# Elementwise work of a two-layer diffusion trunk moved from GpSimd to VectorE and ScalarE

## The chip, the cores and the metric
The kernel runs on one core of a Trainium2 chip. The core has TensorE (PE; its weight loads are PEld), VectorE (DVE), ScalarE (ACT), GpSimd (POOL) and SyncE (SP), which issues most DMAs; each works through its own queue in order. The metric is the device time of one execution in microseconds, and the time shown is the median of three runs.

## The reference
Two layers over 256 context and 256 latent tokens of width 1024. Each layer has four token mixers side by side (gated DeltaNet, S5, HGRN2, retention), each in two directions, then an output projection, a gate, a residual and a layer norm; then a channel mixer, dense SwiGLU in layer 0 and eight experts, two per token, in layer 1. Only latent tokens leave. What the change touches, cut to its core:

```
x  <- LN(alpha*x + gate*sublayer(mod(x)))                # norm, affine g and b
q, k, v = split(silu(short_conv(qkv)));  q = l2norm(q)*64**-.5;  k = l2norm(k)
S5:   lam_bar = exp(lam*step);  h_t = lam_bar*h_(t-1) + b_bar u_t;  y = Re(C h)   # complex
HGRN: att[i,j] = sum_k q[i,k] k[j,k] exp(g[i,k]-g[j,k]),  j <= i
MoE:  out = alpha*x + gate*sum_e w_e * (silu(h w1_e)*(h w3_e)) w2_e
```

## The kernel before
All matrices are fp32 and are multiplied in three passes: a weight arrives by DMA as `wraw`, ScalarE rounds it to `whi` (L390), VectorE or GpSimd subtracts to get `wlo` (L305), and TensorE adds xh*whi, xl*whi and xh*wlo. Tokens lie along the free dimension (512 in layer 0, 256 latent ones in layer 1), features over partitions in tiles of 128.

The stages follow one another: adaLN vectors and the modulated input (`xl`, `xh`); S5 tables, made on the chip from the parameters (`s5_tables`: powers of the step, input weights `s5W`, phases `s5res`, output tables C times a power, stored to DRAM and loaded back); projections and DeltaNet features; S5 states; retention; DeltaNet blocks and chain; HGRN attention by levels; output projection; norm; dense mixer; norm; the same mixers for layer 1; norm; experts. The tables of layer 1 are made beside the first norm.

The order of every engine's queue is set when the program is built: a scheduler walks the instructions by priority, and `tc.high_priority(n)` shifts that of a block. Tiles live in pools, entered and left, and rings of buffers (`bufs`). Names and lines in the rows: L305 is any two-operand product, sum or difference, L317 one with a scalar between, L321 and L323 one with scalars, L329 to L331 ScalarE's functions, L373 a matmul, L386 a weight's DMA. `s5a`, `s5b`, `s5Z`, `s5H` are the S5 states' products, sums and results (L1420 on), two directions one after the other; `hea` the exponents of an HGRN level (L1020 on); `lr`, `lnq`, `lnx` the norm's rows, its Newton step on the inverse root and its affine result; `mlo` the low part of an expert's unit of 1 MB (128x2048); `m_acc` the accumulator of the experts, filled with alpha times the normed rows (`moe_begin`), and `e_sel` the 0/1 matrix that gathers an expert's tokens. A silu is three functions on ScalarE and a last product, which here GpSimd does (L362).

Of the kernel before, what the change touches and what calls it, by code (L numbers as in the profile page):

```python
# [24 lines left out]
P = 128  # L25
# [205 lines left out]
class Trunk:  # L231
# [314 lines left out]
    def gdn_feat(self, l, grp, i, ps, s0, ns):  # L546
# [14 lines left out]
        self.mul(sq, y, y, eng=self.G)  # L561
# [443 lines left out]
    def hgrn_att(self, s, rings):  # L1005
# [8 lines left out]
        for n, sz in enumerate((128, 0) + HLEVELS):  # L1014
            if sz == 0:
                kl = self.t("hkl", [2, 256], bufs=2)
                self.add(kl, kf, kb, eng=self.G)
                ql = q
            else:
# [6 lines left out]
                self.sub(eq[:, :, :, 1], inc[:, :, :, 1], m(0), eng=self.G)  # L1026
                self.sub(eq[:, :, :, 0], m(1), exc[:, :, :, 0], eng=self.G)
# [162 lines left out]
    def s5_tables(self, l):  # L1190
        nc, G = self.nc, self.G
        e = G
# [3 lines left out]
        Ball, Call = n("B", 2, 16, 16), n("C", 3, 16, 16)  # L1196
# [66 lines left out]
        LW, LC = n("LW", 2, 16, 8), n("LC", 2, 16, 8)  # L1263
# [37 lines left out]
        for g0 in range(0, 16, 4):  # L1301
# [4 lines left out]
            sh = [P, 4, 8, 16]  # L1306
            lw = tuple(LW[:, c, gs, :, None].to_broadcast(sh) for c in range(2))
            wb = tuple(bb[:, c, :, None, :].to_broadcast(sh) for c in range(2))
            W = self.t("s5W", [2, 4, 16, 8], bufs=2)
            Wv = W.rearrange("p c g h j -> p c g j h")  # L1310
            tmp, tmq = (self.t(x, [4, 8, 16]) for x in ("s5tmp", "s5tmq"))
            self.cmul((Wv[:, 0], Wv[:, 1]), lw, wb, tmp)
# [16 lines left out]
            lc = tuple(LC[:, c, gs, :, None].to_broadcast(sh) for c in range(2))  # L1329
            cb = tuple(Cm[:, c, :, None, :].to_broadcast(sh) for c in range(3))  # L1330
            Y = self.t("s5W", [2, 4, 16, 8], bufs=2)
            Yv = Y.rearrange("p c g h i -> p c g i h")
            self.mul(Yv[:, 0], lc[0], cb[0], e)
            self.mul(tmq, lc[1], cb[1], e)
            self.sub(Yv[:, 0], Yv[:, 0], tmq, e)
            self.mul(Yv[:, 1], lc[0], cb[2], e)
            self.mul(tmq, lc[1], cb[0], e)
            self.sub(Yv[:, 1], Yv[:, 1], tmq, e)
            nc.sync.dma_start(scm[g0 // 4], Y.rearrange("p c g h i -> p (c g h i)"))
# [731 lines left out]
    def run(self):  # L2071
# [14 lines left out]
        with self.context("B"):  # L2086
            tables = self.s5_tables(1)
# [51 lines left out]
```

## Time and profile before

| | before |
|---|---|
| median of three runs (lowest, highest) | 2537.23 us (2534.49, 2539.19) |
| profiled execution | 2538.93 us, span 2537.1 us |
| busy TensorE | 2273.1 us, 90% |
| busy VectorE | 1735.0 us, 68% |
| busy ScalarE | 1265.9 us, 50% |
| busy GpSimd | 526.0 us, 21%, 494 instructions |
| mean granted TensorE clock | 0.926 |

Stages by time: tables, input and first projections to about 180 us; mixers of layer 0 to 585; norm and layer 1's tables to 642; dense mixer to 1020; norm to 1072; mixers of layer 1 to 1452; norm, router and gather to 1500; experts to 2520; last norm. A share of busy time over the whole span mixes these; what a part is worth is read from its own stretch.

### The profile page before, as it was taken

The page shows a single profiled execution, that of the slowest core. Times are in us where ns is not written, and L with a number is a line of the kernel's source. Part 1 is how long each engine was busy: PE and PEld are TensorE (multiplying, and loading weights), DVE is VectorE, ACT ScalarE, POOL GpSimd, SP SyncE. Part 2 cuts the span into 40 slices and gives each one's busy share as a digit, 9 for nine tenths or more (in the row PEclk, how much of TensorE's full clock was granted, in tenths as well). Part 3 has the DMA queues.
Part 4 walks back from the last instruction along what each step waited for, and adds up shares of the span by engine and source line. Part 5 has one row for each costly group of instructions (what it writes and reads, how often), then busy time and mean ns, then how long its engine had stood idle before and what let it go on. Part 6 is the DMA issues. An engine that isn't in the chain of part 4 may idle for free. (4 is left out here: it accounts for less than half of the span.)

```text
span 2537.1 us, 33303 instructions
## 1 busy us (share of the span) xinstructions
PE 2273.1 (90%) x12928; PEld 1781.8 (70%) x12928; DVE 1735.0 (68%) x2326; ACT 1265.9 (50%) x1459; POOL 526.0 (21%) x494
## 2 busy tenths in 40 slices
PE   3789998878999999789877769999999999999997
PEld 2567666554788887468656558778787878788885
DVE  7646556787533322454566588988888888889887
ACT  1443433322544422533533337767676767677774
POOL 5523433326422200332332230000000000001000
PEclk7889998888999999889987779999999999999998
DMA  7243142415422233652130439989898989899994
GB/s 287 95 154 104 59 172 85 154 57 185 169 99 100 90 126 108 230 168 91 63 122 14 183 142 353 360 311 362 321 366 313 364 322 365 309 358 339 367 361 169
DMA packets 122515, 532.75 MB, mean 210 GB/s; under 512 B 25968, under 2 KB 37232, under 8 KB 78960
## 3 DMA queue, kind: packets, MB, share of 16 engines
q1 hardware_dynamic: 95472, 511.74, 54.8%
q10 hardware_dynamic: 26880, 18.82, 2.5%
q8 instruction: 104, 1.70, 0.3%
q14 instruction: 59, 0.48, 0.1%
HBM read 509.23 MB, written 21.28 MB: 209 GB/s over the span
## 5 line engine op out<-in xcount | busy, mean ns | idle before, releaser
L305 DVE TENSOR_TENSOR mlo<-mraw,mhi 128x2048 fp32r<-128x2048 f32 x333 | 769.8, 2324 | 110.8 <-ACT mhi L390 108.8
L390 ACT CAST mhi<-mraw 128x2048 fp32r<-128x2048 f32 x336 | 639.2, 1906 | 216.0 <-PE psh L373 136.0
L373 PE MATMUL psh<-mlo,e_xh 128*128 128x512 f32 x896 | 358.4, 400 | 6.3 <-DVE mlo L305 6.3
L373 PE MATMUL psh<-mhi,e_xh 128*128 128x512 f32 x896 | 351.7, 395 | 7.8 <-ACT mhi L390 7.8
L373 PE MATMUL psh<-mhi,e_xl 128*128 128x512 f32 x896 | 352.3, 393 | 0.0
L373 PE MATMUL psacc<-xh,whi 128*128 128x512 f32 (+2 forms) x784 | 315.5, 403 | 35.5 <-ACT k2P L329 13.3
L390 ACT CAST whi<-wraw 128x1024 fp32r<-128x1024 f32 x142 | 145.5, 1026 | 352.9 <-PE psacc L373 335.3
L373 PE MATMUL psacc<-xh,wlo 128*128 128x512 f32 (+2 forms) x784 | 309.0, 394 | 9.2 <-DVE wlo L305 9.2
L373 PE MATMUL psacc<-xl,whi 128*128 128x512 f32 (+2 forms) x784 | 308.2, 393 | 6.5 <-DVE xl L305 6.4
L305 DVE TENSOR_TENSOR wlo<-wraw,whi 128x1024 fp32r<-128x1024 f32 x142 | 179.6, 1266 | 194.8 <-ACT whi L390 185.3
L305 POOL TENSOR_TENSOR e_xl<-k2B,e_xh 128x512 fp32r<-128x512 f32 x16 | 31.0, 1946 | 997.5 <-ACT e_xh L1867 997.5
L373 PEld LDWEIGHTS psacc<-xh,whi 128*128 128x128 f32 (+1 forms) x784 | 152.4, 195 | 73.6 <-ACT k2P L329 25.8
L373 PEld LDWEIGHTS psh<-mhi,e_xh 128*128 128x128 f32 x896 | 170.1, 190 | 46.3 <-ACT mhi L390 8.9
L373 PEld LDWEIGHTS psh<-mlo,e_xh 128*128 128x128 f32 x896 | 170.3, 190 | 43.6 <-DVE mlo L305 8.6
L373 PEld LDWEIGHTS psh<-mhi,e_xl 128*128 128x128 f32 x896 | 170.1, 190 | 34.3
L373 PEld LDWEIGHTS psacc<-xh,wlo 128*128 128x128 f32 (+1 forms) x784 | 151.5, 193 | 45.4 <-DVE wlo L305 11.3
L373 PEld LDWEIGHTS psacc<-xl,whi 128*128 128x128 f32 (+1 forms) x784 | 152.0, 194 | 42.4 <-DVE xl L305 8.7
L373 PE MATMUL psy<-mlo,e_gh 128*128 128x512 f32 x448 | 177.0, 397 | 0.0
L373 PE MATMUL psy<-mhi,e_gl 128*128 128x512 f32 x448 | 173.9, 391 | 0.0
L373 PE MATMUL psy<-mhi,e_gh 128*128 128x512 f32 x448 | 160.1, 394 | 0.0
L373 PEld LDWEIGHTS psy<-mhi,e_gh 128*128 128x128 f32 x448 | 84.2, 188 | 20.0 <-ACT e_gh L1846 1.5
L373 PEld LDWEIGHTS psy<-mlo,e_gh 128*128 128x128 f32 x448 | 84.5, 189 | 17.7 <-DVE mlo L305 0.2
(535 smaller groups left out, 3728.0 us busy)
## 6 DMA issues: line engine op xcount, KB each, us to landing
mraw<-in_moe_w_dram SPq DMA_DIRECT2D x336, 1024.0 KB, 6.8
wraw<-in_ada_w_dram SPq DMA_DIRECT2D x80, 512.0 KB, 4.0
wraw<-in_ffn_w_dram SPq DMA_DIRECT2D x60, 512.0 KB, 3.3
wraw<-in_w_feat_dram SPq DMA_DIRECT2D x44, 512.0 KB, 3.4
sraw<-in_ada_w_dram SPq DMA_DIRECT2D x16, 512.0 KB, 9.8
wraw<-in_w_out_dram SPq DMA_DIRECT2D x16, 512.0 KB, 3.6
wraw<-in_w_tok_dram SPq DMA_DIRECT2D x12, 512.0 KB, 3.2
s5w<-s5wt SPq DMA_DIRECT2D x8, 512.0 KB, 2.8
```

Of the source, the lines that this page charges most:

```text
L305: (eng or self.V).tensor_tensor(out=out, in0=a, in1=b, op=op)
L373: self.T.matmul(out, lhsT, rhs, start=start, stop=stop, **k)
L390: self.S.copy(hi, raw)
```

## The change
Nothing that is computed changes; nearly all is where it is done.

- The last product of every silu goes to VectorE; the squares of the DeltaNet q and k go to ScalarE.
- HGRN: two of four subtractions per level, and the `hkl` sum, go to VectorE.
- S5 tables: the phases (`s5res`) are doubled on VectorE; `s5W` is written in memory order, not through a transposed view; the output tables leave the loop for a function of their own, on VectorE, in halves (`s5Y`) with a DMA each, for layer 1 at lower priority (-2000).
- S5 states: both phase products go to VectorE.
- Norms: the four `lr` products that were GpSimd's go to VectorE; the eight affine results to ScalarE.
- Experts: the accumulator's start goes to VectorE in fewer instructions, the first three `mlo` too, at lower priority (-500).

```
-        self.mul(out, out, tmp, eng=self.G)                   # silu
+        self.mul(out, out, tmp)
-        self.mul(sq, y, y, eng=self.G)                        # q and k
+        self.act(sq, y, AF.Square)
-                self.sub(eq[:, :, :, 1], inc[:, :, :, 1], m(0), eng=self.G)
-                self.sub(eq[:, :, :, 0], m(1), exc[:, :, :, 0], eng=self.G)
+                self.sub(eq[:, :, :, 1], inc[:, :, :, 1], m(0))
+                self.sub(eq[:, :, :, 0], m(1), exc[:, :, :, 0])
...
-            self.cmul((pr[:, :, m:2 * m], pi[:, 0, :, m:2 * m]), (pr[:, :, 0:m], pi[:, 0, :, 0:m]), bc, wtmp[:, :, :m], eng=e)
+            self.cmul((pr[:, :, m:2 * m], pi[:, 0, :, m:2 * m]), (pr[:, :, 0:m], pi[:, 0, :, 0:m]), bc, wtmp[:, :, :m])
...
+    def s5_out_tables(self, scm):
+        LC, Call = self.s5y2
+        sh = [P, 4, 16, 8]
+        for g0 in range(0, 16, 4):
+            gs = slice(g0, g0 + 4)
+            lc = tuple(LC[:, c, gs, None, :].to_broadcast(sh) for c in range(2))
+            cb = tuple(Call[:, c, gs, :, None].to_broadcast(sh) for c in range(3))
+            for c, (a, b) in enumerate(((0, 1), (2, 0))):
+                Y = self.t("s5Y", [4, 16, 8])
...
+                self.mul(Y, lc[0], cb[a])
+                self.mul(tmp, lc[1], cb[b])
+                self.sub(Y, Y, tmp)
+                self.nc.sync.dma_start(scm[g0 // 4][:, c * 512:c * 512 + 512], Y.rearrange("p g h i -> p (g h i)"))
...
-            self.mul(c, self.s5pi, z[:, ::-1], eng=self.G)     # states, and again after the scan
+            self.mul(c, self.s5pi, z[:, ::-1])
...
-            self.mul(r[:, k], r[:, k], rs, eng=self.G if k % 4 == 3 else self.V)
+            self.mul(r[:, k], r[:, k], rs)
-            self.ts(x, r[:, k], g[:, k:k + 1], ALU.mult, b[:, k:k + 1], ALU.add, eng=self.G)
+            self.act(x, r[:, k], AF.Identity, scale=g[:, k:k + 1], bias=b[:, k:k + 1])
...
+        self.stt(self.macc, f(self.nh), one, f(self.nl), ALU.mult, ALU.add)
+        for b in range(2):
+            m = self.macc[:, b]
+            self.stt(m, m, ALPHA, rows[0], ALU.mult, ALU.mult)
+            self.stt(m, rows[1], ALPHA, m, ALU.mult, ALU.add)
...
-        early = [self.unit(src, 4, "pool") for src in self.up_srcs(jobs[0][0], 0)[:3]]
+        with self.tc.high_priority(-500):
+            early = [self.unit(src, 4) for src in self.up_srcs(jobs[0][0], 0)[:3]]
```

The engines' queues move with it. VectorE in the startup, before: the second half of the adaLN vectors (`mods`), the modulated input (`sc1p`, `sx`) and the input weights `s5W`.

```order
L305 TENSOR_TENSOR s5tmp_1027<-s5LW_830,s5bb_1019 128x512
L305 TENSOR_TENSOR mods_108<-psP_189,params 128x16
L305 TENSOR_TENSOR s5W_1026<-s5W_1026,s5tmp_1027 128x4x8x16
L321 TENSOR_SCALAR sc1p_197<-mods_108 128x8 x2
L305 TENSOR_TENSOR s5tmp_1077<-s5LW_830,s5bb_1069 128x512
L323 TENSOR_SCALAR sx_200<-sx_200,sc1p_197,mods_108 128x256 x2
L323 TENSOR_SCALAR sx_210<-sx_210,sc1p_197,mods_108 128x256 x2
L323 TENSOR_SCALAR sx_220<-sx_220,sc1p_197,mods_108 128x256 x2
```

VectorE at the same place, now:

```order
L1319 COPY s5cz_920<-s5C_700 64x2x64 x2
L305 TENSOR_TENSOR s5Y_1133<-s5Y_1133,k2B_1134 128x512
L305 TENSOR_TENSOR mods_108<-psP_189,params 128x16
L305 TENSOR_TENSOR s5tmp_1053<-s5LW_833,s5bb_1045 128x512
L305 TENSOR_TENSOR s5wtm_858<-s5res_768,s5wc_861 128x16x8
L321 TENSOR_SCALAR s5wc_861<-s5wc_861 128x16
L305 TENSOR_TENSOR k2B_1152<-s5LC_834,s5C_700 128x512
L321 TENSOR_SCALAR sc1p_197<-mods_108 128x8 x2
L305 TENSOR_TENSOR s5W_1052<-s5W_1052,s5tmp_1053 128x512
L305 TENSOR_TENSOR s5res_768<-s5res_768,s5wtm_858 128x16x8
L305 TENSOR_TENSOR s5wc_861<-s5t_117_709,s5t_118_710 128x16
L305 TENSOR_TENSOR s5res_768<-s5res_768,s5wc_861 128x16x16
```

Phase products (`s5res`, `s5wtm`) and output tables (`s5Y`, `k2B`) now stand between the vectors and the input, and `s5W` is written as a plain 128x512 tile.

VectorE at the first direction's S5 states, before: the products and the scan, with one `kq` (a k tile times its inverse norm), a weight subtraction and DeltaNet's gate (`g_`) between.

```order
L305 TENSOR_TENSOR s5a_1238<-s5res_1164,s5Z_1175 128x1024
L305 TENSOR_TENSOR kq_314<-k2P_488,k2P_492 128x512
L305 TENSOR_TENSOR s5a_1238<-s5a_1238,s5b_1239 128x1024
L1427 SCALAR_TENSOR_TENSOR s5Z_1175<-s5rm_1172,s5a_1238 128x1024
L305 TENSOR_TENSOR wlo_1552<-wraw_1550,whi_1553 128x1024
L305 TENSOR_TENSOR g_x_626<-gab_586,params 128x32
L321 TENSOR_SCALAR g_x_626<-g_x_626 128x32
L305 TENSOR_TENSOR s5Z_1175<-s5res_1164,s5Z_1175 128x1024
L321 TENSOR_SCALAR g_z_628<-g_y_627 128x32
L305 TENSOR_TENSOR s5H_1237<-s5Z_1175,s5b_1239 64x32x31 x2
L581 RECIPROCAL g_z_628<-g_z_628 128x32
L305 TENSOR_TENSOR s5last_1250<-s5Z_1175,s5b_1239 128x32
```

VectorE now, at the second direction's first products (`s5last` ends the first direction):

```order
L305 TENSOR_TENSOR s5last_1266<-s5Z_1191,s5b_1255 128x32
L305 TENSOR_TENSOR wlo_1492<-wraw_1490,whi_1493 128x1024
L305 TENSOR_TENSOR kq_314<-k2P_441,k2P_445 128x512
L305 TENSOR_TENSOR s5lx_1268<-s5last_1266,s5res_1180 128x32
L305 TENSOR_TENSOR s5ly_1269<-s5last_1266,s5res_1180 128x32
L1444 COPY s5H_1253<-s5last_1266 64x32 x2
L305 TENSOR_TENSOR s5Z_1192<-s5Z_1192,s5lx_1268 128x32
L305 TENSOR_TENSOR s5Z_1192<-s5Z_1192,s5ly_1269 128x16 x2
L305 TENSOR_TENSOR s5a_1275<-s5res_1180,s5Z_1192 128x1024
L305 TENSOR_TENSOR s5b_1276<-s5res_1180,s5Z_1192 128x1024
L317 SCALAR_TENSOR_TENSOR k2P_535<-psacc_504,params,k2P_535 128x2x255
L305 TENSOR_TENSOR k2P_488<-k2P_488,k2P_492 128x512
```

The `s5b` products, which GpSimd did, are in VectorE's row, and the last silu product of a k tile (`k2P_488`) stands behind both directions' first products.

VectorE in the norm ahead of the experts, before: statistics (`lnst`, `lnmv`, `lnv`) and the Newton step.

```order
L1572 BN_STATS lnst_11350<-lr_11344 128x6
L305 TENSOR_TENSOR lnAB_11424<-lnAB_11424,mods_109 128x8
L1572 BN_STATS lnst_11371<-lr_11344 128x6 x2
L1573 BN_AGGR lnmv_11349<-lnst_11350 128x2
L1573 BN_AGGR lnmv_11370<-lnst_11371 128x2
L321 TENSOR_SCALAR lnv_11355<-lnmv_11349 128x1
L321 TENSOR_SCALAR lnv_11376<-lnmv_11370 128x1
L305 TENSOR_TENSOR lnq_11356<-lnrs_11354 128x1
L305 TENSOR_TENSOR lnq_11377<-lnrs_11375 128x1
```

VectorE there now:

```order
L1577 BN_STATS lnst_11382<-lr_11376 128x6
L305 TENSOR_TENSOR lnAB_11456<-lnAB_11456,mods_109 128x8
L305 TENSOR_TENSOR mlo_11548<-mraw_11419,mhi_11549 128x2048
L1577 BN_STATS lnst_11403<-lr_11376 128x6 x2
L1578 BN_AGGR lnmv_11381<-lnst_11382 128x2
L305 TENSOR_TENSOR mlo_11552<-mraw_11421,mhi_11553 128x2048
L305 TENSOR_TENSOR mlo_11556<-mraw_11423,mhi_11557 128x2048
L1578 BN_AGGR lnmv_11402<-lnst_11403 128x2
L321 TENSOR_SCALAR lnv_11387<-lnmv_11381 128x1
L321 TENSOR_SCALAR lnv_11408<-lnmv_11402 128x1
L305 TENSOR_TENSOR lnq_11388<-lnrs_11386 128x1
L305 TENSOR_TENSOR lnq_11409<-lnrs_11407 128x1
```

The three `mlo` stand between the statistics; the accumulator's three steps (`m_acc`) are over a hundred rows further down, between the first expert's weight subtractions.

## Rows read from the trace of the kernel before
The columns of a timeline are start and length in us, engine, line, operation, output and inputs, partitions x elements, how many, and in brackets the idle time before it and what ended it.

**Rows 1.** Windows; columns: stretch, length, busy PE, PEld, DVE, ACT, POOL, clock, DMA.
```profile
60.00:120.00 60.00, 40.75 (x176) 32.34 (x173) 40.73 (x44) 29.51 (x58) 35.23 (x28) 0.80 0.29 107
180.00:600.00 420.00, 367.41 (x3067) 273.06 (x3065) 275.78 (x654) 144.55 (x268) 158.53 (x180) 0.89 0.31 105
660.00:1020.00 360.00, 360.00 (x1576) 292.70 (x1574) 112.67 (x122) 126.58 (x166) 66.61 (x44) 1.00 0.30 104
1080.00:1440.00 360.00, 303.36 (x2675) 235.11 (x2668) 206.39 (x386) 139.45 (x262) 103.78 (x121) 0.85 0.28 93
1440.00:1500.00 60.00, 28.95 (x124) 21.34 (x123) 47.31 (x114) 13.32 (x20) 31.70 (x11) 0.65 0.46 182
1500.00:2520.00 1020.00, 1002.86 (x4553) 821.30 (x4552) 892.20 (x590) 710.20 (x484) 30.45 (x16) 0.99 0.89 335
```

**Rows 2.** Timeline of TensorE and ScalarE's queue: start, length, what, [wait, releaser].
```profile
82.14 0.80 PE L373 MATMUL psacc<-xl,whi 128*128 128x512 f32 x1 [5.27 <-DVE xl L305]
103.30 0.79 PE L373 MATMUL psacc<-xh,whi 128*128 128x512 f32 x1 [3.99 <-ACT k2P L329]
149.64 0.76 PE L373 MATMUL psacc<-xh,whi 128*128 128x512 f32 x1 [8.61 <-DVE s5rm L1397]
176.83 0.48 PE L373 MATMUL psacc<-xh,whi 128*128 128x512 f32 x1
...
139.50 6.50 ACTq L1382 DMA_DIRECT2D s5U<-s5u  x2
```

**Rows 3.** Timeline of VectorE, startup.
```profile
37.62 0.69 DVE L305 TENSOR_TENSOR s5tmp<-s5LW,s5bb 128x512 f32<-128x512 f32 x1
...
67.35 1.76 DVE L305 TENSOR_TENSOR s5tmp<-s5LW,s5bb 128x512 f32<-128x512 f32 x1
...
89.23 3.88 DVE L305 TENSOR_TENSOR xl<-sx,xh 128x512 fp32r<-128x512 f32 x4
```

**Rows 4.** Timeline of GpSimd, startup.
```profile
66.46 2.10 POOL L305 TENSOR_TENSOR s5W<-s5W,s5tmq 128x512 f32<-128x512 f32 x1
```

**Rows 5.** Timeline of VectorE and TensorE in the first norm.
```profile
629.91 6.26 DVE L305 TENSOR_TENSOR lr<-lr,lnrs 128x512 f32<-128x512 f32 x6
628.88 1.09 PE L1317 MATMUL psB<-consts,s5W 128*128 128x128 f32 x4 [5.93 <-DVE s5W L305]
```

**Rows 6.** Timeline of VectorE and GpSimd at the S5 states.
```profile
177.63 1.23 DVE L305 TENSOR_TENSOR s5a<-s5res,s5Z 128x1024 f32<-128x1024 f32 x1 [0.99 <-ACT s5Z L329]
182.86 2.29 DVE L1427 TENSOR_TENSOR_SCAN s5Z<-s5rm,s5a 128x1024 f32<-128x1024 f32 x1
191.30 2.39 DVE L305 TENSOR_TENSOR s5H<-s5Z,s5b 64x992 f32<-64x992 f32 x2
177.68 3.46 POOL L305 TENSOR_TENSOR s5b<-s5res,s5Z 128x1024 f32<-128x1024 f32 x1 [6.29 <-ACT s5Z L329]
```

**Rows 7.** Timeline of VectorE, GpSimd and TensorE at the start of the experts.
```profile
1464.32 4.49 DVE L305 TENSOR_TENSOR lnq<-lnq,lnv 128x1 f32<-128x1 f32 x2
1487.51 4.67 DVE L321 TENSOR_SCALAR e_sel<-consts,m_pos 128x128 fp32r<-128x128 f32 x2
1505.72 2.29 DVE L305 TENSOR_TENSOR mlo<-mraw,mhi 128x2048 fp32r<-128x2048 f32 x1 [2.22 <-ACT mhi L390]
1454.85 13.87 POOL L305 TENSOR_TENSOR mlo<-mraw,mhi 128x2048 fp32r<-128x2048 f32 x3
1489.93 0.48 PE L1769 MATMUL psA<-consts,e_sel 128*128 128x128 f32 x1 [7.17 <-DVE e_sel L321]
```

**Rows 8.** Timeline of VectorE and GpSimd at HGRN levels.
```profile
482.36 2.73 DVE L305 TENSOR_TENSOR hea<-hp 128x256 f32<-128x256 f32 x4 [4.44 <-PE psA L373]
515.96 0.74 DVE L305 TENSOR_TENSOR hea<-hp 128x256 f32<-128x256 f32 x2
482.47 3.11 POOL L305 TENSOR_TENSOR hea<-hp 128x256 f32<-128x256 f32 x4 [7.29 <-PE psA L373]
514.87 1.19 POOL L305 TENSOR_TENSOR hea<-hp 128x256 f32<-128x256 f32 x2 [5.05 <-PE psB L373]
```

More of the change, by code (lines that the diff above doesn't have):

```diff
@@ L1016, in hgrn_att @@
                 kl = self.t("hkl", [2, 256], bufs=2)
-                self.add(kl, kf, kb, eng=self.G)
+                self.add(kl, kf, kb)
                 ql = q
@@ L1188, in cmul, with s5_tables @@
         self.add(out[1], out[1], tmp, eng)
-    def s5_tables(self, l):
-        nc, G = self.nc, self.G
-        e = G
+    def s5_tables(self, l, ypool):
+        nc = self.nc
         v = lambda k: self.Pm(k).rearrange("p (l g) -> p l g", l=DEPTH)[:, l]
@@ L1305, in s5_tables @@
             self.cmul((bb[:, 0], bb[:, 1]), (B[:, 0], B[:, 1]), qb, bb[:, 2])
-            sh = [P, 4, 8, 16]
-            lw = tuple(LW[:, c, gs, :, None].to_broadcast(sh) for c in range(2))
-            wb = tuple(bb[:, c, :, None, :].to_broadcast(sh) for c in range(2))
+            sh = [P, 4, 16, 8]
+            lw = tuple(LW[:, c, gs, None, :].to_broadcast(sh) for c in range(2))
+            wb = tuple(bb[:, c, :, :, None].to_broadcast(sh) for c in range(2))
             W = self.t("s5W", [2, 4, 16, 8], bufs=2)
-            Wv = W.rearrange("p c g h j -> p c g j h")
-            tmp, tmq = (self.t(x, [4, 8, 16]) for x in ("s5tmp", "s5tmq"))
-            self.cmul((Wv[:, 0], Wv[:, 1]), lw, wb, tmp)
+            self.cmul((W[:, 0], W[:, 1]), lw, wb, self.t("s5tmp", [4, 16, 8]))
             wt = self.t("s5wt", [2, 4, P], bufs=2)
@@ L1328, in s5_tables @@
             self.act(kfb[:, :, gs], pk, AF.Copy)
[L1329 to L1339, printed above, removed]
         T = [self.t("s5wt", [8, 16, 8], bufs=2) for _ in range(2)]
@@ L1353, in s5_tables @@
             nc.sync.dma_start(sT[:, 8 * h:8 * h + 8], T[h])
+        self.s5y2 = LC, Call
         return sr, sw, scm, sT
+    def s5_out_tables(self, scm):
+        LC, Call = self.s5y2
+        sh = [P, 4, 16, 8]
+        for g0 in range(0, 16, 4):
[4 more added lines that the diff above has]
+                Y = self.t("s5Y", [4, 16, 8])
+                with self.context("B"):
+                    tmp = self.s2().rearrange("p (g h i) -> p g h i", g=4, h=16)
+                self.mul(Y, lc[0], cb[a])
+                self.mul(tmp, lc[1], cb[b])
+                self.sub(Y, Y, tmp)
+                self.nc.sync.dma_start(scm[g0 // 4][:, c * 512:c * 512 + 512], Y.rearrange("p g h i -> p (g h i)"))
     def s5_phases(self, res):
@@ L1882, in moe_begin @@
         rows = [self.t(f"e_x{c}1", [D]) for c in "hl"]
-        f = lambda t: t.bitcast(F32)
-        self.add(self.macc, f(self.nh), f(self.nl), eng=self.G)
         for j, nm in enumerate(("ln_g", "ln_b")):
             self.nc.scalar.dma_start(rows[j], self.A[nm][1, 0:1, :].to_broadcast([P, D]))
-            for b in range(2):
-                m = self.macc[:, b]
-                self.tt(m, m, rows[j], ALU.mult if j == 0 else ALU.add, eng=self.G)
-        self.ts(self.macc, self.macc, ALPHA, ALU.mult)
+        f = lambda t: t.bitcast(F32)
+        one = f(self.t("e_gl", [4, P], F32R, bufs=2))[:, 0, 0:1]
+        self.V.memset(one, 1.0)
+        self.stt(self.macc, f(self.nh), one, f(self.nl), ALU.mult, ALU.add)
[3 more added lines that the diff above has]
+            self.stt(m, rows[1], ALPHA, m, ALU.mult, ALU.add)
     def experts(self, jobs, first=False):
@@ L2000, in mixers @@
         if tables is None:
+            y = self.enter("taby", "right")
             self.enter("tab", "right")
-            tables = self.s5_tables(l)
-            self.leave("tab", "start")
+            tables = self.s5_tables(l, y)
+            self.leave("tab")
+            self.mx = y
+            self.s5_out_tables(tables[2])
+            self.leave("taby", "start")
         self.enter("sP", "left")
@@ L2084, in run @@
         self.leave("l0")
+        y = self.enter("taby", "right")
         self.enter("tab", "right")
         with self.context("B"):
-            tables = self.s5_tables(1)
+            tables = self.s5_tables(1, y)
         self.leave("tab")
+        self.mx = y
+        with self.tc.high_priority(-2000):
+            self.s5_out_tables(tables[2])
         for p in (0, 1):
```

8 lines of the change are left out of this document (4 added, 4 removed).

## The prediction

> **What bounds the kernel now.** I read the stretches of the span first. TensorE is busy all 360 us of the dense channel mixer (660 to 1020 us) and 1002.86 of 1020 us of the expert body, so nothing that other engines do less of there is worth more than the 17 us missing in the second [rows 1]. That leaves the mixers, the norms and the start of the experts. The reader is to see in [rows 1] how far TensorE falls short there: 19.25 of 60 us between 60 and 120, 52.59 of 420 between 180 and 600, 31.05 of 60 between 1440 and 1500. Next comes what ends its waits: `xl` of VectorE before the first projection, then an eviction on ScalarE, then 8.61 us before the last product of the DeltaNet features [rows 2]. The profile names VectorE's `s5rm` as the releaser of the last; it is a memset of the state masks, while ScalarE stood at the issue of the `s5U` DMAs from 139.50 to 146.04 [rows 2], and I take these to be the cause.
>
> Then I compared one and the same VectorE instruction with GpSimd silent and with GpSimd working [rows 3]: the 128x512 product `s5tmp` takes 0.69 us at 37.62, where GpSimd pauses, and 1.76 at 67.35, where GpSimd is in its table products [rows 4]; the last four subtractions `xl`, of the same shape, take 3.88 together, 0.97 each [rows 3]. So GpSimd's work is paid twice: once on GpSimd, once in VectorE's longer instructions.
>
> **Startup (0 to 180 us).** VectorE's order from the last copy of the powers (27.5 us) to the last `xl` holds, in the new order, 44 instructions of 512 elements at 0.62 us pitch (27.3), 64 of 16 to 128 elements (10.5), 15 of 256 (5.0) and two weight subtractions (2.3): 45.2 us with no wait, against 65.5 us from 27.5 to the end of the last `xl` at 93.0 now [rows 3] (0.62 is the 0.69 of `s5tmp` less the 0.07 by which neighbours overlap). The same count of the old order gives 37.6; the 28 us on top are waits of some 4 us and the doubling of [rows 3]. If GpSimd is silent, as it is in the new order from its first memsets to the retention tables, the last `xl` stands near 73.5 and the first near 66, and TensorE's first projection, held by `xl` until 82.14, begins some 16 us sooner. The 3.99 us before 103.30 go as well, since the retention tables on ScalarE no longer collide with the eviction. Third projection: near 83 instead of 103.30 [rows 2], that is 20 us.
>
> Part of it goes back. The S5 states run wholly on VectorE in the new order and stand ahead of the last silu product of the last k tile, whose square ScalarE and whose sum of squares TensorE want next. For one direction that is four 128x1024 products and sums and one more pair (1.23 each), a scan (2.29) and the two outputs (2.39) [rows 6], then a weight subtraction, a `kq`, small ones, and two products of the other direction: 16.5 us. TensorE has one projection (5.3 us) and a transpose to do meanwhile; the sum of squares behind it then waits about 12 us, and the first output of the states a further 3. The 8.61 us shrink to about 2. By walking TensorE's new order with the durations of before, the fourth group's first product starts near 163 us instead of 176.83 [rows 2], and 5.5 us of the state outputs that now lie far behind it are done by then: 19 us. Ends: 10 (the wait at the norm twice as long) and 27 (the wait hidden).
>
> **First norm (600 to 642 us).** The table products of layer 1 lie beside the norm on GpSimd. Of VectorE's `lnq` pair, s5cz copies, and six `lr` products (6.26 for six, 1.04 each [rows 5]) about 6 us are there only because GpSimd works beside them; TensorE's wait of 5.93 us for `s5W` [rows 5] ends. Against this stand 16 half tables more on VectorE (48 x 0.62 over the whole kernel, half of it here), in gaps. The adaLN weights still have to arrive, and they end not far behind. I take 7 us; ends 2 (only the DMA counts) and 11.
>
> **Start of the experts (1440 to 1500 us).** Three `mlo` on GpSimd hold 13.87 us, and inside it two one-column products of VectorE take 4.49 us; later GpSimd's sums for the accumulator stand beside two `e_sel` of 4.67 [rows 7]. Now the three `mlo` go to VectorE at 2.29 each, 6.9 us, placed between the statistics, but the stretched one-column work (9 us more than its size, the 4.49 of two products the largest part) shrinks to about 1: `ln_n` comes 2.5 us sooner. The accumulator work lies later, after the first units, so `e_sel` follows the count at once: 6 of the 7.17 us of TensorE's wait go [rows 7], and a us at the next `e_sel`. Sum 9.5, less half a us for six 1.2 to 2.3 us instructions that now stand between weight subtractions in the body, where VectorE is busy 892.20 of 1020 us [rows 1]: 9. Ends 4 and 12.
>
> **HGRN levels.** Each level moves two subtractions of 128x256 from GpSimd to VectorE, 42 in three calls. Alone two take 0.74 us on VectorE. At 515.96 GpSimd had done its pair already (514.87 to 516.06), so VectorE's pair was last, and with four it is 0.74 us later; and TensorE's next matmuls wait for `hea` [rows 8]. At 482.36 both work together: VectorE's four take 2.73 and GpSimd's four 3.11, while eight on VectorE alone would take 2.96: nothing lost [rows 8]. I take six levels that lose, 4 us; ends 0 and 10.
> The Trainium skill ("SBUF — State Buffer", section "Who interferes with whom") says that VectorE with two SBUF inputs and a GpSimd instruction that reads SBUF lock one another out for a whole instruction. The pair at 482.36 agrees in the sum. By that rule no level could lose, and this term would be 0 instead of 4; 515.96 shows a level at which there was no overlap to be won, so I keep the 4.
>
> **Edits at nothing.** The 22 silu products of the dense mixer: TensorE is full there [rows 1], VectorE busy 112.67 of 360 us. The other silus and the squares: 1.3 us on GpSimd against 0.62 on VectorE or ScalarE, hidden by projections except at the first and last tile; without that cover a us each way. Eight `lnx` at 0.6 us on ScalarE between the casts of the second norm: 4 us lost at most, and 3 us of wait for GpSimd won; I take zero, ends -4 and +4. The S5 states of layer 1: the latent part alone, where GpSimd's 3.4 us products lie inside the chain as in layer 0 [rows 6]; between 6 won and 12 lost, and I take zero, since projections follow.
>
> **Sum.** 19 + 7 + 9 - 4 = 31 us. The profiled execution took 2538.93 us (span 2537.1 and 1.8 around it), which gives 2508; the median is 1.7 us lower, so 2506 to 2508, and I say 2507. With all ends on one side (10 + 2 + 4 - 10 = 6 and 27 + 11 + 12 + 0 = 50) it would be 2532 and 2488; the ends are hardly all met together.
>
> **Rivals.** (1) Larger gain: what [rows 3] shows happens in every mixer stage. TensorE is idle 53 us from 180 to 600 and 57 from 1080 to 1440 [rows 1]; if a quarter goes, another 27 us, 2480. For it: GpSimd is busy 158.53 and 103.78 us in these stretches [rows 1], in pieces beside VectorE. Against it: most waits there are dependence chains with ScalarE or TensorE, which VectorE does not shorten. (2) No gain: GpSimd's help was real. The waits at the norm and the states become 25 us and not 15, HGRN loses 10, and norm and expert start give their low ends: 19 - 10 + 2 + 4 - 10 = 5, and layer 1 takes back the rest: 2535. For it: VectorE is busy 47.31 of 60 us at the start of the experts [rows 1] and takes 42 subtractions, three `mlo` and all tables on top, in one queue. (3) Slower, by one mechanism: VectorE's single queue at the S5 states. If each of the two directions, not only the first, stands before a product that TensorE wants next, layer 0 waits 27 us where I take 15, and layer 1, whose order has the same chain, 27 where I take nothing: 31 - 12 - 27 = -8, 2547. It decides as soon as these waits, both layers together, pass 46 us. Against it: the projections of the retention features are independent and were written behind the states, and 5 us of each chain is covered. That the change doesn't do what it says can't be: 202 of GpSimd's 424 rows remain.
>
> The Trainium skill ("Perfetto Trace Analysis", section "Optimizing Scalar/DVE Operations") warns that moving work between these two engines might not help, because they share a read port. Read as a mechanism here, GpSimd's and VectorE's times add up already, and the move gives only the difference of the engines' speeds: of the three `mlo`, 13.87 us against 6.9 [rows 7]. That is a gain too, and rival 2 is what would be left if only VectorE's share counted.
>
> **Chances.** Forecast 0.63, rival 1 0.18, rival 2 0.11, rival 3 0.08. A measurement of this kernel tells 0.2%, 5 us, from no change. Forecast and rival 1 lie beyond it on the fast side, and rival 2 for half its chance: faster 0.86; the other half, 0.05, same; rival 3 with the tail of rival 2 slower, 0.09. The range for 8 in 10 reaches over rival 1's centre and stops before rival 2's: 2479 to 2532; the forecast's own is 2488 to 2527.
>
> **What would show it.** Right: `s5tmp` and `xl` at 0.69 us everywhere in the first 100 us; the first projection with `xl` near 66 us; a new wait of 10 to 15 us on TensorE near 135 to 150 whose releaser is ScalarE's square after VectorE's k product; `lnq` of one column at 0.2 us before the experts; `e_sel` within 2 us of the count. Wrong: TensorE's first projection after 75 us; waits of over 20 us behind `s5H`; HGRN levels over a us longer; TensorE short of 58 of 60 us in the expert body.

## The result, and the profile after

The changed kernel took 2474.57 us (median of four executions, 2472.9 to 2482.76) against 2538.21 (2534.49 to 2543.03): a ratio of 0.9751 [0.9732, 0.977], 63 us where 31 were forecast, and 4 us below the range. Run again later it took 2478.9 (six executions, 2474.04 to 2490.9), ratio 0.9757 [0.974, 0.9773]. The ten have their median at 2477.2, from which losses are counted below. The direction was right and the gain twice the forecast: most of the terms worked out from waits came near, those put at nothing did not.

The first lines of the page of after, the clock slices with them:
```profile
span 2470.8 us, 33235 instructions
PE 2262.0 (92%) x12928; PEld 1777.8 (72%) x12928; DVE 1735.4 (70%) x2558; ACT 1278.3 (52%) x1483; POOL 234.8 (10%) x238
...
PEclk8989997789999999889978799999999999999998
```
GpSimd's busy time fell from 526.0 to 234.8 us, and VectorE, which took most of that work (2326 instructions became 2558), is busy as long as before, 1735.0 then. This is the surprise of the page: the time of the added work came back, mostly from shorter old instructions.

Windows of after, with the columns of [rows 1] (the same stretches, though each stage now begins earlier):
```profile
60.00:120.00 60.00, 59.03 (x272) 48.99 (x272) 36.84 (x66) 40.94 (x86) 6.82 (x8) 0.93 0.65 213
180.00:600.00 420.00, 378.96 (x3066) 270.02 (x3065) 285.23 (x755) 154.13 (x288) 73.96 (x91) 0.89 0.35 119
660.00:1020.00 360.00, 354.76 (x1530) 276.56 (x1529) 135.43 (x175) 135.79 (x194) 32.65 (x18) 0.99 0.38 124
1080.00:1440.00 360.00, 297.35 (x2645) 234.69 (x2644) 226.73 (x522) 140.02 (x248) 72.31 (x85) 0.83 0.30 100
1440.00:1500.00 60.00, 58.61 (x278) 48.05 (x278) 57.20 (x44) 42.15 (x30) 0.00 (x0) 1.00 0.88 321
```
The 19 us that TensorE lacked between 60 and 120 us are down to 1 (3.7 in the second trace); the 31 us between 1440 and 1500 are gone because that stretch is now the expert body.

The same group of VectorE instructions in the trace of before and then of after (count, least/median/longest ns, first and last start, form):
```profile
L305 DVE TENSOR_TENSOR xl<-sx,xh x8: 677/1083/2079, 80.6 to 92.4; 128x512 fp32r<-128x512 f32 x8
L305 DVE TENSOR_TENSOR s5W<-s5W,s5tmp x16: 1072/1120/2431, 36.5 to 636.1; 128x512 f32<-128x512 f32 x16
L305 DVE TENSOR_TENSOR hea<-hp x48: 404/426/1492, 412.4 to 1414.2; 128x256 f32<-128x256 f32 x48
```
```profile
L305 DVE TENSOR_TENSOR xl<-sx,xh x8: 679/681/682, 64.6 to 71.3; 128x512 fp32r<-128x512 f32 x8
L305 DVE TENSOR_TENSOR s5W<-s5W,s5tmp x16: 681/682/686, 36.2 to 580.0; 128x512 f32<-128x512 f32 x16
L305 DVE TENSOR_TENSOR hea<-hp x96: 402/416/622, 385.2 to 1359.0; 128x256 f32<-128x256 f32 x96
```
The longest says more than the median: `xl` and `s5W` are not stretched any more (part of `s5W` is its new layout: its least was 1072), and the longest `hea` takes 0.62 us for 1.49. Of all two-operand VectorE instructions of 128x512 before 1500 us in the trace of before, `s5W` left out, 89 with no GpSimd instruction beside them have a mean of 0.69 us, and 50 with one 0.99; half of the 50 are no longer than alone. Taken over all shapes up to 1500 us, every excess over the median of the like that stands alone (`s5W` against itself), VectorE lost 121 us that way before and 21 after.

TensorE's waits of after that answer to [rows 2, 7] (start, length, instruction, [wait, releaser]):
```profile
65.31 0.80 PE L373 MATMUL psacc<-xl,whi 128*128 128x512 f32 x1
121.59 2.49 PE L373 MATMUL psA<-s5U,s5tabwc 128*128 128x64 f32 x16 [1.83 <-DMA s5tabwc<-s5w]
143.20 2.08 PE L373 MATMUL psP<-k2P,consts 128*128 128x512 f32 x2 [11.39 <-ACT k2P L329]
1409.72 1.62 PE L1945 MATMUL psA<-consts,ln_n 128*128 128x128 f32 x6 [14.26 <-DVE ln_n L323]
1423.93 0.48 PE L1774 MATMUL psA<-consts,e_sel 128*128 128x128 f32 x1 [1.01 <-DVE e_sel L321]
```
The first `xl` product starts at 65.31 (forecast near 66), and the one new wait stands where and as long as forecast: 11.39 us at 143 (10.7 in the second trace), behind the square. How it comes about is seen on VectorE and, below, on ScalarE:
```profile
137.07 0.68 DVE L305 TENSOR_TENSOR kq<-k2P,k2P 128x512 f32<-128x512 f32 x1
...
138.87 1.23 DVE L305 TENSOR_TENSOR s5a<-s5res,s5Z 128x1024 f32<-128x1024 f32 x1
140.01 1.22 DVE L305 TENSOR_TENSOR s5b<-s5res,s5Z 128x1024 f32<-128x1024 f32 x1
141.14 0.74 DVE L317 SCALAR_TENSOR_TENSOR k2P<-psacc,params,k2P 128x510 f32<-128x510 f32 x1
141.80 0.68 DVE L305 TENSOR_TENSOR k2P<-k2P,k2P 128x512 f32<-128x512 f32 x1
```
```profile
142.51 0.63 ACT L329 ACTIVATE k2P<-k2P 128x512 f32<-128x512 f32 x1 [2.25 <-DVE k2P L305]
```
The silu's last product (141.80) stands behind the states' phase products, ScalarE's square waits for it, and TensorE for the square.

Where the time came from, by the places at which TensorE passes the same matmul in each trace (us; gains against before; the second trace of after is its slowest execution, 2490.9, the first its fastest, 2472.9; of before there is one trace):
```
stretch of the span                     forecast   after   after again
start to the last `ra` product              19      24.6       19.0
then to the first norm                      -4       0.6       -4.1
first norm and dense mixer                   7      12.8       12.8
second norm to layer 1's `s5U`               0       1.0        2.2
layer 1's mixers to the last `hatt`          0      17.8        9.6
third norm to the first `e_sel`              9       9.2        9.2
expert body                                  0       0.3       -0.4
sum                                         31      66.3       48.3
```

### The profile page after: what moved, and what is told of

Its sections match the earlier page's. It is cut to its first block, busy times and chain, and to the rows that moved or that the text cites. A ratio compares the mean times of both kernels' runs of the same rounds, so it can differ in the third digit from the quotient of the medians.

```text
span 2470.8 us, 33235 instructions
## 1 busy us (share of the span) xinstructions
PE 2262.0 (92%) x12928; PEld 1777.8 (72%) x12928; DVE 1735.4 (70%) x2558; ACT 1278.3 (52%) x1483; POOL 234.8 (10%) x238
## 5 line engine op out<-in xcount | busy, mean ns | idle before, releaser
L305 DVE TENSOR_TENSOR wlo<-wraw,whi 128x1024 fp32r<-128x1024 f32 x142 | 172.1, 1212 | 167.5 <-ACT whi L390 165.4
```

What stands on the lines that cost most here:

```text
L305: (eng or self.V).tensor_tensor(out=out, in0=a, in1=b, op=op)
```

## The experiments

All times are medians; differences under about 10 us are not read as effects, for a reason that the second group shows. Theory A: GpSimd's activity by itself costs time, by what it does to VectorE beside it, so a quiet GpSimd is what won. Theory D: a saved wait also leaves TensorE's clock up. Against them stands the prediction's own reading, that each part is worth the waits it ends; other rivals are named where they come up.

**The parts undone, one at a time, in the kernel after.** Each puts the products of one place back on GpSimd:
```diff
-            self.mul(c, self.s5pi, z[:, ::-1])            # u_states, and the product of r
+            self.mul(c, self.s5pi, z[:, ::-1], eng=self.G)
-        self.mul(out, out, tmp)                           # u_silu, and sq on GpSimd
+        self.mul(out, out, tmp, eng=self.G)
-                self.add(kl, kf, kb)                      # u_hgrn, and both eq differences
+                self.add(kl, kf, kb, eng=self.G)
-                self.mul(Y, lc[0], cb[a])                 # u_tables, and tmp, sub, the phases
+                self.mul(Y, lc[0], cb[a], self.G)
-            self.act(x, r[:, k], AF.Identity, scale=g[:, k:k + 1], bias=b[:, k:k + 1])   # u_norm, and every 4th r*rs
+            self.ts(x, r[:, k], g[:, k:k + 1], ALU.mult, b[:, k:k + 1], ALU.add, eng=self.G)
```


> The changed kernel with the S5 states' phase products back on GpSimd. The prediction's step (they cost 12 us of wait at the norm and 3 at the outputs in layer 0): 2462 to 2470, faster, as the wait near 143 us goes. Theory A: 2478 to 2485 (eight GpSimd products of 3 us stretch VectorE again in layer 1's S5 stage as in layer 0's). Theory B: 2480 to 2490, in layer 1 above all.

2505.26 us, ratio to before 0.986 [0.9836, 0.9884]: 28 us lost.

> The changed kernel with the last silu products and the squares of q and k back on GpSimd. The prediction counted them as nothing: 2473 to 2477. Theory B (chains): 2482 to 2495, since a silu and a square lie in every DeltaNet feature's chain and each is 0.6 us slower, before the gates and the readouts too. Theory A: 2478 to 2485, as the instructions are few beside VectorE's.

2509.2, 0.9879 [0.9855, 0.9904]: 32 lost.

> The changed kernel with the HGRN subtractions back on GpSimd. The prediction's step (two engines at a level save time): 2468 to 2472. Theory A (sharing wins nothing, and it stretches others): 2476 to 2482. Theory C: anything within 5 us.

2497.19, 0.9826 [0.9798, 0.9853]: 20 lost, though the prediction had counted this part as a cost.

> The changed kernel with the phases and output tables of S5 back on GpSimd (still in the new layout and in halves). The prediction's step: 2490 to 2500, as 16 us of the startup and 5 to 9 of the first norm are lost. If the layout and the halves did most, 2475 to 2482.

2511.65, 0.989 [0.9874, 0.9905]: 34 lost. The first `xl` product comes at 71.0 us, so 11 of the 17 us there are order and layout, 6 the engine (one trace).

> The kernel after the change with the norms' last pass back on GpSimd (every fourth product with the reciprocal, and the scaled copies lnx). The prediction gave the first norm 7 us, from the table products of layer 1 that no longer lie beside it, and the copies nothing, 4 us at most either way. If that is right: 2476 to 2484, and the stretch from the norm's first matmul to the end of the dense mixer 451 to 455 us. If GpSimd's work beside the norm is what counts, whichever it is: 456 to 462 us there, 2484 to 2492.

2497.96, 0.9827 [0.9802, 0.9852]: 21 lost, but not where the edit is: first norm and dense mixer take 450 us, as in after (451), so the copies are worth nothing there, as forecast. With the tables undone that stretch takes 460. In its trace 7.5 us are lost against after's first trace already at the first norm, ahead of the edit; the rest shows in the second norm (71 us against 67 and 65) and in layer 1's mixers (351 against 333 and 342), where this kernel does on each engine what after does.

All five lie above every range that was stated, the prediction's and the theories'. The five losses add to 135 us, over twice the whole, and the experts' start and the tables' layout were not undone at all. So the parts do not add up.

**How much is noise.** Three groups of independent neighbours are written the other way round, on GpSimd the two key products of each block; and the kernel after once more:
```diff
-            self.mul(rw[d], kt, hd(self.egc), eng=self.G)
-            self.mul(kd[d], kt, hd(self.ekd), eng=self.G)
+            self.mul(kd[d], kt, hd(self.ekd), eng=self.G)
+            self.mul(rw[d], kt, hd(self.egc), eng=self.G)
```


> The kernel after the change with three groups of independent neighbours written in the other order: the four differences of each HGRN level, the first two products of each output-table piece, and the two key products of each gated-delta block on GpSimd. Nothing moves to another engine. Theory A (GpSimd's own activity is what costs time): the same as after, 2474 within 5 us. Rival L (the gain is a lucky order, and any new order loses some of it, which would also explain why the undone parts alone cost 31 + 34 + 23 us, more than the 63 of all): off by 10 us or more, to either side.

> The kernel after the change as it is, once more, on the chip of the three runs beside it. If the 12 us by which the run with swapped neighbours lay above it is the spread of executions and chips: 2472 to 2486, ratio 0.974 to 0.978. If that order cost something: 2470 to 2476 again.

2486.8 (0.9779 [0.9746, 0.9811]) and 2478.9. The medians are 8 to 10 us apart, but the intervals overlap, and the kernel after varies by 18 us over its ten executions: no cost of the swap is shown. The swap and the second set of after ran on two chips; another kernel (quiet_rest, below) took the same on both, so the chips are hardly the reason. Hence the bound above.

One trace says still less about a stage. u_norm and ghost1 (below) give VectorE, ScalarE and GpSimd the instructions of after in the same order up to the first norm, yet TensorE passes the last `ra` product at 262.3 and 275.5 us, where after's two traces have 259.0 and 264.5. Their windows from the first `xl` product to the last `gy`, first of u_norm, then of ghost1:
```profile
65.50:397.60 332.10, 301.44 (x2515) 232.01 (x2514) 191.48 (x364) 135.84 (x265) 68.42 (x83) 0.90 0.35 115
```
```profile
65.40:405.60 340.20, 309.97 (x2514) 236.09 (x2515) 192.27 (x364) 136.18 (x266) 69.21 (x83) 0.89 0.35 112
```
After's two (shown in the next group) take 323 and 335 us there, with TensorE busy 294 and 301. So the same queues (two TensorE products stand elsewhere in ghost1) give stretches 17 us apart, nearly all of it in TensorE's busy time.

And a rival stands that no run holds fixed: order. The scheduler sorts anew after every other edit, however local. In layer 1's mixers, of some 400 VectorE instructions that a run shares with the kernel it was made from, 52 to 74 stand in another order in every run of the first, third and fourth group, 60 of them in u_norm, whose edit lies in the norms; over the whole kernel it is 75 (u_norm) to 257 (u_three). The swap, by contrast, left VectorE's queue as it was by names. The undone parts therefore measure engine and order together.

**From the other side: parts of the change in the kernel before,** silus and squares alone (b_silu), then with the states and HGRN (b_eng), and the complement, after with these three undone (u_three):

> The kernel before with one part of the change alone: silu products on VectorE, squares of q and k on ScalarE. Taking that part out of the changed kernel cost 31 us. If the parts add up, 2508. If what counts is that GpSimd is quiet, one part alone helps little, as the tables, states and norms stay: 2528 to 2538. The prediction's nothing: 2540.

> The kernel before with three parts of the change, all of them moves to another engine without a new order: silus and squares, the S5 states' phase products, the HGRN differences. Silus and squares alone gave 5 us. Theory A (what counts is that GpSimd is quiet, so the parts together give more than one by one): 25 to 45 us faster than before, 2496 to 2516, most of it in the mixer stages of both layers. Rival P (each part is worth its own small gain, and the rest of the 63 is the S5 tables' place and order): 2522 to 2534.

> The kernel after the change with three engine moves undone together: silu products and squares, the S5 states' phase products, the HGRN differences are back on GpSimd; the tables on VectorE with their new place, both norms and the experts' start stay changed. It is the other half of the run that made only these three moves in the kernel before and won 6 us. If the two halves add up (rival P): after less those 6 us, 2480 to 2490. If each half is worth little without the other (theory A, more exactly: layer 0 has two chains, the tables and the mixers, and the longer one decides): 2500 to 2515, with the startup still at 65 us to the first xl product, norm 1 and the dense mixer still at 451 us, and the loss in layer 0 up to the gates (10 to 20 us) and in layer 1's mixers (10 to 15 us).

2535.83 (0.9979 [0.9957, 1.0001]), 2534.03 (0.9975 [0.9961, 0.9989]) and 2509.86 (0.9885 [0.9867, 0.9903]). This is the clearest finding. The tables, norms and the experts' start alone win 31 us; the three engine moves alone win 6 (silus and squares alone nothing that is clear of no change); both win 63. The same three moves are worth 6 us in the kernel before and 33 on top of the rest. b_eng lies at the slow end of rival P's range and far from theory A's; u_three lies where theory A put it and far from rival P. So neither is right in both: the halves need each other, but not because the three moves do something large alone. The moves came with a new order in both kernels: 182 of VectorE's 2326 instructions stand elsewhere in b_eng, though it was meant to have none.

Where the three moves went in the kernel before is seen in the windows from the first `xl` product to the last `gy`, and of layer 1's mixers, of before, then of that run:
```profile
82.10:415.40 333.30, 301.29 (x2542) 230.36 (x2544) 185.00 (x328) 132.96 (x258) 119.57 (x118) 0.93 0.34 111
1083.70:1434.80 351.10, 296.56 (x2636) 231.28 (x2636) 203.90 (x382) 135.39 (x254) 102.41 (x119) 0.84 0.27 91
```
```profile
82.30:419.90 337.60, 316.61 (x2538) 244.00 (x2538) 190.00 (x350) 135.13 (x262) 81.03 (x90) 0.87 0.34 110
1092.90:1425.60 332.70, 283.82 (x2636) 222.38 (x2636) 206.79 (x416) 137.12 (x257) 63.20 (x82) 0.88 0.29 95
```
In these two traces TensorE's idle time in layer 0 fell from 32 to 21 us, as it should, but its busy time rose from 301 to 317 for the same matmuls, at a granted clock of 0.87 for 0.93; the second group showed 16 us of difference in busy time for the very same queues. In layer 1 the moves gave 18 us, of it 13 in busy time. The same windows of after (its first trace) and of its second:
```profile
65.30:388.30 323.00, 293.92 (x2521) 226.45 (x2522) 192.71 (x365) 136.22 (x266) 69.17 (x83) 0.93 0.36 118
1044.70:1378.00 333.30, 288.60 (x2636) 228.98 (x2636) 207.60 (x416) 137.74 (x257) 68.19 (x82) 0.86 0.30 96
```
```profile
65.20:400.40 335.20, 300.96 (x2515) 230.98 (x2514) 191.90 (x364) 136.19 (x266) 69.23 (x83) 0.91 0.35 114
1053.80:1395.30 341.50, 295.52 (x2638) 235.63 (x2638) 207.59 (x416) 138.87 (x257) 68.09 (x82) 0.83 0.28 94
```
Two executions of one program differ by 7 us of busy time in each stretch, with the clock.

**GpSimd's activity added, no engine's work moved.** Useless squarings of just-made tiles, on GpSimd, into a scratch tile that nobody reads, at the places of the change (all; only up to layer 1's mixers; only from there):
```diff
+    def ghost(self, *srcs):
+        for x in srcs:                       # as 2-D; ghost0, ghost1: only in their layers
+            for o in range(0, x.shape[1] - 255, 256):
+                self.mul(self.gh, x[:, o:o + 256], x[:, o:o + 256], self.G)
...
         self.mul(out, out, tmp)
+        self.ghost(out)
```


> The changed kernel, with GpSimd doing work that nobody uses: after each silu, each square, each HGRN level, each pair of S5 phase products and each norm product it squares 256 elements at a time of the tile just made, into a scratch tile, about as much as it did there before the change (the tables and the experts' start are left without). Theory A (GpSimd's mere activity stretches VectorE's instructions, in all mixers): 2500 to 2515, that is 25 to 40 us of the 63 given back, with VectorE's 128x512 products back above 1 us beside it. Theory B (GpSimd's slow instructions stood in chains, and only their own length counted): 2475 to 2483, since nobody waits for the ghosts. Theory C (the scheduler found a better order): 2475, the order being nearly the same.

> The kernel after the change with the useless GpSimd squarings everywhere but in layer 1's mixers and norm 3: the other half of the set. All of them cost some 40 to 50 us, those of layer 1 alone about 10. Theory A (each squaring costs where it runs, and layer 1 is dear only when it is entered badly): this half costs 20 to 30 us up to layer 1's first projection, 2495 to 2510 in all, and layer 1 itself takes 5 us more or less than in the kernel after. Theory E (layer 1's loss is handed on from layer 0): 2515 to 2528, with 20 us or more of it lost behind layer 1's first projection, though no squaring runs there.

> The kernel after the change with the useless GpSimd squarings of the earlier run only from layer 1's mixers on (silus, squares, states, HGRN levels, norm 3); layer 0 and both first norms are those of after. Theory A as a local effect: nothing is lost up to layer 1's first S5 projection at 1044.7 us, and from there the 29 us that the full set of squarings lost behind that place (its 55.1 at e_sel less its 25.9 at the projection), so 2495 to 2506 in all, with VectorE's instructions longer in that layer alone. Rival E (layer 1 gains because it is entered in a better state, with the clock up, not for what GpSimd does in it): under 8 us lost, 2475 to 2482.

2524.33 (0.9927 [0.9905, 0.9949]), 2510.6 (0.9874 [0.9839, 0.9909]) and 2488.49 (0.9781 [0.9748, 0.9813]): 47, 33 and 11 us lost, the last not clear of after. So a kernel with all of this useless work on GpSimd loses three quarters of what the change won, more than theory A allowed for. How is not shown. Where the loss lies in the traces is not where the squarings are. Layer 1's mixers in ghost1, with squarings, then in ghost0, without:
```profile
1064.90:1407.30 342.40, 291.67 (x2636) 231.47 (x2636) 211.02 (x416) 137.62 (x257) 108.32 (x136) 0.86 0.28 93
```
```profile
1066.00:1418.90 352.90, 305.90 (x2634) 239.40 (x2634) 207.93 (x415) 135.64 (x254) 63.08 (x82) 0.82 0.27 87
```
With squarings the stretch takes 342 us, as in after (333 and 342); without them 353. And ghost1 enters it at 1064.9 us, as late as ghost0 (1066.0; after 1044.7 and 1053.8), with only two of its 56 squarings ahead of it, 1.5 us before. Theory A's local effect therefore fails in layer 1, rival E gains a point from ghost0, and that 33 and 11 add up to 44 of 47 may be luck. Three more things are not separated: the squarings re-sorted VectorE's queue (188 of 2558 instructions in the full set); a squaring holds its tile's buffer until it has read it; and VectorE's stretching grew by 28 us only (from 21 to 49), while TensorE was busy 35 us longer for the same matmuls (2297.0 against 2262.0, mean clock 0.922 against 0.935).

**The clock after a wait.** Thirty useless matmuls behind layer 1's S5 projection, where TensorE waits, in the kernel with HGRN undone and in the kernel before:
```diff
         self.proj_feat(l, C_SU, u)
+        if l == 1:
+            d = self.ps("B")
+            for _ in range(30):
+                self.mm(d, self.xh[:, 7, 0:P], self.xh[:, 7])
```


> The kernel with the HGRN subtractions back on GpSimd, and 30 matmuls of no use (layer 1's input by itself, 512 columns) put into TensorE's queue behind the S5 projection of layer 1, where it waits 10.7 us for ScalarE. In that kernel TensorE then worked full 30 us at a granted clock of 0.50. If the clock is what this stretch lost against the changed kernel (theory D: lost waits are paid twice, once idle and once at the lower clock level after them), the time falls from 2497 by 8 to 15, to 2482 to 2489, with the clock near 1 behind the S5 projection. If the order of instructions is what it lost (theory C), it stays at 2497 or gets 2 to 5 longer by the matmuls.

> The kernel before with the same 30 matmuls of no use at the same place. It waits 9.36 us there and works 73 us behind it at a mean granted clock of 0.82, where the changed kernel has 0.87. Theory D: 2530 to 2535, 4 to 9 less. Theory C or A: 2540, no change.

2493.55 (0.9816 [0.9798, 0.9833]) and 2535.71 (0.998 [0.9968, 0.9992]): 4 and 5 us, the first with overlapping intervals. The first lies between the ranges of both theories, the second at the edge of theory D's, and the matmuls re-sorted VectorE's queue as well (60 and 54 instructions). In their traces the granted clock over the 72 us from layer 1's first `s5U` product is 0.83 in both, against 0.74 in u_hgrn and 0.82 in before. Not settled: work put into that one wait buys little.

**More of the same.** The readouts, rotary products, retention tables, gate weight and the FFN's low halves off GpSimd too (quiet_rest, run twice), and then the gated-delta products as well (quiet_all):
```diff
-        self.mul(m, m, z[:, :, t], eng=self.G)
+        self.mul(m, m, z[:, :, t])
-            self.sub(gl[f], h, gh[f].bitcast(F32), eng=self.G)
+            self.sub(gl[f], h, gh[f].bitcast(F32))
...
-                             self.egl[hp, c, 2 * s + bl, d, :, None].to_broadcast([64, 2, 64]), eng=self.G)
+                             self.egl[hp, c, 2 * s + bl, d, :, None].to_broadcast([64, 2, 64]))
```


> The kernel after the change with more work taken off GpSimd: the readouts' last products, the rotary products of q and k, the retention tables' sums, the gates' norm weight and the FFN's low halves on VectorE, the squares of the readout and of the GELU on ScalarE. Theory A: VectorE takes some 70 us of work and its other instructions shrink again, 2460 to 2472. Rival B (what the change gained was the places in the queues, and VectorE is now the one that is waited for): no gain or a loss, 2475 to 2492.

> The run with the readouts, rotary products, retention tables, gate weight and FFN low halves off GpSimd, once more, beside the kernel after. Theory A: faster than that one by 4 to 10 us, 2464 to 2472. Rival B (its first time was the spread): within 3 us of the kernel after.

> As the run before, and the gated-delta rule's products (gates, decays, the decayed state of every step) on VectorE too: GpSimd then holds little but the memsets and the experts' low halves. Theory A: 2450 to 2468. Rival B: the 64 decayed-state products now stand in VectorE's queue in the middle of the chain of steps, and the gated-delta stages grow: 2480 to 2505.

2470.29 (0.9723 [0.9694, 0.9753]), 2470.32 (0.9726 [0.9699, 0.9753], 8.6 us below the kernel after beside it, intervals overlapping) and 2485.02 (0.9781 [0.9752, 0.981]). The first is the best version here, by a margin that these runs don't quite prove; the gated-delta products should stay on GpSimd.

## Why the prediction came out too small

- **Startup, 19 us: right.** 24.6 and 19.0 (21.2 in u_norm and 8.0 in ghost1, with the same queues). Its steps came out one by one: the first `xl` at 65.31, the wait of 11.39 us, and in place of the 8.61 us at the last product [rows 2] a wait of 1.83 on an output table. Of the further 3 us at the states' first output 0.57 came.
- **HGRN, -4 us: wrong in sign for the whole kernel.** The levels on VectorE are as short as forecast, four subtractions in 1.43 us where two took 0.74 [rows 8]; they are 48 that moved, not 42:
```profile
457.16 1.43 DVE L305 TENSOR_TENSOR hea<-hp 128x256 f32<-128x256 f32 x4 [3.99 <-PE psA L373]
```
  Layer 0 behind the retention gave 0.6 and -4.1 us, which fits; but undone the part costs 20, engine and order together, and no trace shows where. The rule in the Trainium skill ("SBUF — State Buffer", "Who interferes with whom"), which would have set this term to 0, lies nearer to that than the row that the prediction kept; neither has the 20.
- **First norm, 7 us: mis-sized, 12.8.** The tables carry it, as said: undone, the stretch is 9 us longer. TensorE's idle time in norm and dense mixer went from 15 to 4 us; the forecast had counted the `s5W` wait and six `lr` [rows 5] and not the other waits of the norm.
- **Experts' start, 9 us: right in the sum.** 9.2; on VectorE:
```profile
1402.96 4.43 DVE L305 TENSOR_TENSOR mlo<-mraw,mhi 128x2048 fp32r<-128x2048 f32 x2
...
1408.28 0.28 DVE L305 TENSOR_TENSOR lnq<-lnq,lnv 128x1 f32<-128x1 f32 x2
...
1423.59 0.48 DVE L321 TENSOR_SCALAR e_sel<-consts,m_pos 128x128 fp32r<-128x128 f32 x2
```
  `lnq` went from 4.49 to 0.28 us and `e_sel` from 4.67 to 0.48 [rows 7]. The 6 us at the first `e_sel`, though, were read from a wait that not every execution has; in b_silu, whose experts start as in before, it is short:
```profile
1485.40 0.47 PE L1769 MATMUL psA<-consts,e_sel 128*128 128x128 f32 x1 [0.83 <-DVE e_sel L321]
```
  There the time is lost later: from the last `hatt` product to the end of the span before, b_silu and b_eng all take 1100 to 1101 us, after 1091 and 1092 (warm_b, the kernel before with matmuls ahead of this, 1096).
- **"Edits at nothing" and layer 1 at zero: this is the step that failed.** The prediction costed silus, squares, states and HGRN at -4 us together; on top of the rest they gave 33 (u_three against after). Layer 1's mixers gave 9.6 to 17.8 us where nothing was counted, and the three moves alone give 18 there in the kernel before (one trace). The norms' last pass, put at zero with ends of -4 and +4, cost 21 undone. The prediction had a likely cause in hand (VectorE stretched beside GpSimd) and used it only where it saw a wait end with a stretched instruction; the rest it dismissed as "dependence chains with ScalarE or TensorE, which VectorE does not shorten". In place of the -4 the runs show a gain of 33 us for these moves on top of the rest, of 6 without it, and 47 us of loss for GpSimd work that nobody reads. Whether the moves win by less stretching, by buffers that come free sooner, by the new order or by the clock stays open.
- **TensorE's own time was held constant.** For the same 12928 matmuls it was busy 2273.1 us before, 2262.0 and 2271.7 in the two traces of after, and 2297.0 in ghost, with the granted clock. The sum had no term for it.
- **Rivals.** The first, 2480 us by relief in every mixer stage, came nearest the time; its relief shows in layer 1 and the norm, not in layer 0 behind the startup, and that its 27 us came so near is partly luck, as the cause is open. The second and third fall: no wait on the states passes 11.39 us. The warning in the Trainium skill ("Perfetto Trace Analysis", "Optimizing Scalar/DVE Operations") that such a move might not help is not borne out: VectorE's busy time did not grow, and 63 us were won.

Still open: why the three moves are worth 6 us in the one kernel and 33 in the other, and what sets layer 1's 331 to 365 us for the same matmuls. u_norm and ghost0 do there on each engine what after does, in another order, and take 351 and 353 us for 333 and 342: order, or the spread between executions, is as large as the losses to be explained. A run that moves engines and keeps every queue's order is missing.

## What to carry to other kernels

Where one VectorE instruction takes twice its least time beside GpSimd, work out the stretching over the whole trace (each instruction against its like that stands alone), and don't put a part at nothing because no wait ends with it. The sum is a warning and no forecast: it fell by 100 us here for 63 won, by 35 in b_eng (121 to 86) for 6, and grew by 28 in ghost for 47 lost. Don't add up parts that were undone one by one: here they came to over twice the whole, so make a run with each half as well. Compare the queues of a run with those of the kernel it was made from before calling its edit local. Run the same program several times before reading a stage difference of under 20 us.

## What the runs showed of the hardware

The granted clock can drop while TensorE shows no wait. In b_eng TensorE was busy all 25 us from 182 to 207, at 1.00, and from 210 to 215 it ran at 0.50, the 1.2 GHz level, without a wait (windows, then two timeline rows of four matmuls of the same form):
```profile
182.00:207.00 25.00, 25.00 (x147) 20.91 (x146) 23.79 (x44) 6.71 (x11) 0.00 (x0) 1.00 0.32 99
...
210.00:215.00 5.00, 5.00 (x25) 5.00 (x25) 0.00 (x0) 0.00 (x0) 0.00 (x0) 0.50 0.57 157
```
```profile
210.34 1.06 PE L373 MATMUL psA<-s5H,s5tabwc 128*128 128x64 f32 x4
...
220.21 0.61 PE L373 MATMUL psA<-s5H,s5tabwc 128*128 128x64 f32 x4
```
What it ran from 207 on are products of 64 columns. A saved wait need thus not be a saved microsecond. And a quiet GpSimd is no end in itself: in quiet_all its busy time before 1500 us is 11 us, from 203 in after, and the kernel was not faster.
